# Piece sizes, half loads and an earlier first store in a DMA-bound DoRA forward kernel

## Chip, cores, metric

One NeuronCore of a Trainium2 chip. The metric is device microseconds of one execution. Before: 162.53 us, the median of 6 runs (162.31 to 163.03).

## The reference

```python
W_adapted = W + scale * (lora_A @ lora_B)          # 256 x 256, rank 16
W_norm = np.sqrt(np.sum(W_adapted ** 2, axis=0, keepdims=True) + 1e-8)
W_final = W_adapted / W_norm * m
y = x.reshape(-1, 256) @ W_final                   # x: 16 x 2048 x 256 float32
```

33.5 MB of x come in, 33.5 MB of y go out. The small algebra on W takes the first microseconds.

## The kernel before

x is 64 groups of 512 rows (J = 4 rows in each of 128 partitions, 4 KB of a partition). Eight groups are a block of 4 MB. There are eight blocks, but SBUF has room for five (XBUFS = 5). ScalarE writes a group's result over its x. So the program loads five blocks, then stores three (freeing three buffers), loads the last three, and stores the rest. Loads go out on SyncE's queue, stores on ScalarE's. For each pair of groups GpSimd rounds x to bf16 (`xb`), TensorE transposes it (`turned`), VectorE copies it out (`xt`), TensorE multiplies (`product`) and ScalarE copies the result (`x_sb<-y_ps`).

```python
    loads = [(0, 2), (2, 2), (4, CH - 4)] + units[1 : XBUFS - 1]    # (first group, groups)
    loads += [((XBUFS - 1) * CH, CH - 3)]
    loads += [(XBUFS * CH - 3 + c, 1) for c in range(3)] + units[XBUFS:]
    ...
    F = NBLK - XBUFS                                # 3
    G = F * CH                                      # 24
    stores = [(b * CH, CH, 21 + b) for b in range(F - 1)]           # (first group, groups, due after group)
    stores += [(G - CH, CH // 2, 24), (G - CH // 2, CH // 2, 24)]
    FIRST = len(stores)
    stores += [(G + c, 1, G + 3) for c in range(4)]
    stores += [(G + 4, CH - 4, 47)]
    ...
    for n in range(len(loads)):                     # SyncE
        if loads[n][0] == XBUFS * CH:
            for k in range(HALF + 1):               # wait for the stores that free the buffers
                nc.sync.wait_ge(sem(f"store{k}"), 16)
        ...
        load_x(n)
    ...
        if p == REST:                               # GpSimd pauses at pair 15
            nc.gpsimd.wait_ge(sem(f"store{HALF}"), 16)
```

"A piece" below is what one partition moves in one run of a DMA: a load of a whole block has pieces of 32 KB, one of a single group 4 KB. A DMA over 128 partitions is 128 pieces (1280 packets of 32 KB for the ten DMAs of whole blocks), 8 for each of the 16 DMA engines.

## Time and profile before

| | before |
|---|---|
| span of the profile | 161.3 us |
| DMA bytes, mean rate | 67.42 MB, 418 GB/s |
| busiest compute engine (PE) | 59% |
| rate while only loads or only stores run | 431 to 432 GB/s |
| first store issued, first store packet | 48.53 us, 52.63 us |

The row to look at is the DMA row of the page: it is at 8 or 9 from the second slice to the last but one. Then only two kinds of loss are left: a DMA engine that is idle, and bytes that move slower than 432 GB/s. The prediction shows the lines for both. Two more views of the kernel before are needed later. The timeline of its start (start us, duration us, engine, line, operation, tiles):

```profile
13.76 2.45 DVE L234 TENSOR_TENSOR w_final<-wam,rnorm 128x256 bf16<-128x256 f32 x2
13.82 2.11 POOL L197 CAST xb<-x_sb 128x2048 bf16<-128x2048 f32 x1 [2.43 <-DMA x_sb<-in_x_dram]
16.13 1.21 DVE L238 COPY xt<-xt_ps 128x1024 f32<-128x1024 f32 x1
...
18.60 0.63 PE L316 MATMUL y_ps<-w_final,xt 128*128 128x256 bf16 x2
```

and the issue of the first store, on ScalarE's queue:

```profile
48.53 0.37 ACTq L149 DMA_DIRECT2D out_dram<-x_sb  x1
```

The weights are ready at 16.2 us, the first product starts at 18.60. w_final takes 2.45 us because it collides with a cast of GpSimd.

### The profile page before, as it was taken

The numbers are of one execution on the slowest core, as the hardware profiler recorded it, in microseconds if no ns is written. First come the engines' busy times: TensorE is split into PE (matmuls) and PEld (weight loads), VectorE is DVE, ScalarE is ACT, GpSimd is POOL, SyncE is SP. The second block draws the span as 40 slices with busy tenths as digits, with TensorE's granted clock in tenths as the row PEclk, the third lists the DMA queues.
The fourth block names the chain that finished last, engine by engine and source line by source line (L and its number), as shares of the span: only waits on it lengthen the run. The fifth ranks groups of instructions, "written<-read, shape, count | busy, mean of one in ns | idle before, by whom it ended". The sixth has DMA issues, their size and how long they took to land. (4 is left out here: it accounts for less than half of the span.)

```text
span 161.3 us, 2012 instructions
## 1 busy us (share of the span) xinstructions
PE 95.2 (59%) x786; PEld 83.8 (52%) x786; DVE 46.6 (29%) x44; ACT 63.9 (40%) x67; POOL 62.9 (39%) x39
## 2 busy tenths in 40 slices
PE   0491899999999700000199999999999940000000
PEld 0160799999998600000179989989899930000000
DVE  0439635353635300000033535353445300000000
ACT  3010076868686520000027675856776850000000
POOL 1085339776764000000674479198676200000000
PEclk9999999999999995555559999999999998555555
DMA  4999999999899999989999999999999999999995
GB/s 163 427 455 459 390 504 406 390 488 423 374 412 361 511 423 390 473 374 451 427 482 414 386 463 421 407 433 433 422 484 419 406 479 414 400 479 423 386 443 228
DMA packets 4356, 67.42 MB, mean 418 GB/s; under 512 B 625, under 2 KB 642, under 8 KB 1666
## 3 DMA queue, kind: packets, MB, share of 16 engines
q1 hardware_dynamic: 2160, 33.82, 49.5%
q10 hardware_dynamic: 2194, 33.59, 48.7%
q14 instruction: 2, 0.02, 0.0%
HBM read 33.85 MB, written 33.55 MB: 418 GB/s over the span
## 5 line engine op out<-in xcount | busy, mean ns | idle before, releaser
L256 ACT COPY x_sb<-y_ps 128x1024 f32<-128x1024 f32 x64 | 62.0, 1014 | 60.0 <-PE y_ps L316 57.8
L197 POOL CAST xb<-x_sb 128x2048 bf16<-128x2048 f32 x32 | 60.4, 1900 | 61.3 <-DMA out_dram<-x_sb 27.7
L316 PE MATMUL y_ps<-w_final,xt 128*128 128x256 bf16 x512 | 63.6, 278 | 1.2 <-PEq L291 1.1
L238 DVE COPY xt<-xt_ps 128x1024 f32<-128x1024 f32 x32 | 39.2, 1224 | 72.6 <-PE xt_ps L302 72.6
L316 PEld LDWEIGHTS y_ps<-w_final,xt 128*128 128x128 bf16 x512 | 51.1, 100 | 8.5 <-issue 1.9
L302 PE MATMUL xt_ps<-identity,xb 128*128 128x128 f32 x264 | 37.0, 287 | 28.2 <-PEq L291 28.2
L302 PEld LDWEIGHTS xt_ps<-identity,xb 128*128 128x128 f32 x264 | 31.7, 148 | 30.3 <-issue 30.0
L283 PE MATMUL y_ps<-sq,ones 128*128 128x256 f32 x4 | 2.1, 674 | 1.6 <-DVE sq L223 1.6
L272 PE MATMUL y_ps<-identity,a_nat 128*16 128x128 f32 x2 | 0.6, 394 | 4.1 <-DMA a_nat<-in_lora_A_dram 4.1
L248 ACT ACTIVATE norm<-y_ps,eps_col 128x256 f32<-128x256 f32 x1 | 0.5, 473 | 5.8 <-PE y_ps L283 5.8
L234 DVE TENSOR_TENSOR w_final<-wam,rnorm 128x256 bf16<-128x256 f32 x2 | 2.5, 1266 | 0.0
L283 PEld LDWEIGHTS y_ps<-sq,ones 128*128 128x128 f32 x4 | 1.2, 326 | 2.3 <-DVE sq L223 2.1
L272 PEld LDWEIGHTS y_ps<-identity,a_nat 128*16 128x16 f32 x2 | 0.1, 88 | 4.1 <-issue 4.1
L246 ACT ACT_TABLE_LOAD x1 | 1.3, 1283 | 2.4 <-issue 2.4
L203 POOL MEMSET xb<- 128x2048 bf16 x1 | 1.8, 1804 | 0.7 <-PE xt_ps L302 0.7
L231 DVE RECIPROCAL rnorm<-norm 128x256 f32<-128x256 f32 x1 | 1.7, 1747 | 0.0
L225 DVE COPY m_all<-y_ps 128x256 f32<-128x256 f32 x1 | 0.4, 424 | 3.3 <-PE y_ps L288 3.3
L214 DVE CAST b_bf<-b_nat 16x256 bf16<-16x256 f32 x1 | 0.3, 281 | 3.5 <-DMA b_nat<-in_lora_B_dram 3.5
L288 PE MATMUL y_ps<-m_row,ones 1*128 1x256 f32 x2 | 1.2, 706 | 0.0
L276 PE MATMUL y_ps<-b_bf,aT 16*128 16x256 bf16 x2 | 0.6, 404 | 0.7 <-DVE aT L216 0.7
L219 DVE SCALAR_TENSOR_TENSOR wa<-y_ps,w_nat 128x512 f32<-128x512 f32 x1 | 0.7, 692 | 0.8 <-PE y_ps L276 0.8
L288 PEld LDWEIGHTS y_ps<-m_row,ones 1*128 1x128 f32 x2 | 0.5, 308 | 0.6 <-issue 0.6
(13 smaller groups left out, 3.3 us busy)
## 6 DMA issues: line engine op xcount, KB each, us to landing
x_sb<-in_x_dram SPq DMA_DIRECT2D x5, 4096.0 KB, 26.5
out_dram<-x_sb ACTq DMA_DIRECT2D x5, 4096.0 KB, 22.7
out_dram<-x_sb ACTq DMA_DIRECT2D x5, 2048.0 KB, 29.0
x_sb<-in_x_dram SPq DMA_DIRECT2D x3, 2048.0 KB, 31.4
x_sb<-in_x_dram SPq DMA_DIRECT2D x1, 2560.0 KB, 44.8
x_sb<-in_x_dram SPq DMA_DIRECT2D x2, 1024.0 KB, 6.1
out_dram<-x_sb ACTq DMA_DIRECT2D x4, 512.0 KB, 50.1
x_sb<-in_x_dram SPq DMA_DIRECT2D x3, 512.0 KB, 46.4
```

The costliest lines, as they stand in the source:

```text
L197: nc.gpsimd.tensor_copy(out=xb_bufs[p % NXB][:], in_=x_bufs[b % XBUFS][:, 2 * c * J : 2 * (c + 1) * J, :],).then_inc(sem("rounded"), 1)
L203: nc.gpsimd.memset(xb_bufs[NPR % NXB][:], 0.0).then_inc(sem("rounded"), 1)
L219: nc.vector.scalar_tensor_tensor(out=wa[:], in0=ab_ps, scalar=float(scale), in1=w_nat[:], op0=ALU.mult, op1=ALU.add).then_inc(dv, 1)
L231: nc.vector.reciprocal(out=rnorm[:], in_=norm[:]).then_inc(dv, 1)
L234: i = nc.vector.tensor_mul(out=w_final[:, t], in0=wam[:, t], in1=rnorm[:])
L238: nc.vector.tensor_copy(out=xt_bufs[p % NXT][:].rearrange("p r t -> p (r t)").bitcast(FP32), in_=xt_ps[p % 2][:],).then_inc(sem("copied"), 1)
L246: nc.scalar.activation(out=warm[:], in_=eps_col[:], func=AF.Sqrt)
L256: nc.scalar.copy(out=x_bufs[b % XBUFS][:, c * J : (c + 1) * J, :], in_=y_ps[g % 2][:]).then_inc(sem("room"), 1)
L283: i = nc.tensor.matmul(n2_ps, ones[:], sq[:, t, :], start=(t == 0), stop=(t == KC - 1))
L288: nc.tensor.matmul(mb_ps, ones[0:1, :], m_row[:], start=True, stop=True).then_inc(pe, 1)
L302: i = nc.tensor.transpose(xt_ps[p % 2][:, j * P : (j + 1) * P], xb_bufs[p % NXB][:, j, :].bitcast(FP32), identity[:],)
L316: i = nc.tensor.matmul(y_ps[h][:, j, :], xt_bufs[p % NXT][:, r : r + P, t], w_final[:, t, :], start=(t == 0 and (j % (J // 2)) == 0), stop ...
```

## The change

The intent: compute starts earlier (the first pair is rounded by ScalarE, m is broadcast before the norm, GpSimd stays out of VectorE's way), so that the first store can be issued earlier; loads arrive in halves so that compute waits less; and at the two places where loads and stores meet, one side is cut into 2 KB pieces so that it trickles between the large pieces of the other side. The diff, cut to its core (waits and helper functions left out):

```diff
-    loads = [(0, 2), (2, 2), (4, CH - 4)] + units[1 : XBUFS - 1]
-    loads += [((XBUFS - 1) * CH, CH - 3)]
-    loads += [(XBUFS * CH - 3 + c, 1) for c in range(3)] + units[XBUFS:]
+    H = XBUFS * CH
+    loads = [(0, 2, 2 * J), (2, 2, 2 * J), (4, 4, 4 * J), (8, 4, 4 * J), (12, 4, 4 * J)]
+    loads += [(b * CH, CH, CH * J) for b in range(2, XBUFS - 1)]
+    loads += [(H - CH, 4, 4 * J), (H - 4, 4, 2)]          # third number: rows of a piece, 1 KB each
+    loads += [(g0, 4, 4 * J) for g0 in range(H, NCH - 4, 4)]
+    loads += [(NCH - 4, 2, 2 * J), (NCH - 2, 2, 2 * J)]
-    stores = [(b * CH, CH, 21 + b) for b in range(F - 1)]
-    stores += [(G - CH, CH // 2, 24), (G - CH // 2, CH // 2, 24)]
+    stores = [(b * CH, CH, CH * J, 20 + b) for b in range(F - 1)]
+    stores += [(G - CH, 3, 3 * J, G - 1), (G - 5, 1, J, G - 1), (G - 4, 4, 4 * J, G - 1)]
-    stores += [(G + c, 1, G + 3) for c in range(4)]
-    stores += [(G + 4, CH - 4, 47)]
+    stores += [(G, 4, 2, G + 3), (G + 4, CH - 4, (CH - 4) * J, 49)]
...
-    for p in range(NPR):                                   # GpSimd
+    for p in range(1, NPR):
...
-        if p == 0:
-            nc.gpsimd.wait_ge(sem("dve"), 4)
+        if p == 1:
+            nc.gpsimd.wait_ge(sem("dve"), 6)
+        if p == 2:
+            nc.gpsimd.wait_ge(sem("dve"), 8)
...
+    nc.vector.wait_ge(dv, 8)
+    nc.vector.sem_inc(sem("room"), 2)                      # was done by TensorE
...
+    wait_load(nc.scalar, 0)
+    nc.scalar.copy(out=xb_bufs[0][:], in_=x_bufs[0][:, 0 : 2 * J, :]).then_inc(sem("early"), 1)
...
+    nc.tensor.matmul(mb_ps, ones[0:1, :], m_row[:], start=True, stop=True).then_inc(pe, 1)   # moved ahead of n2
     nc.tensor.wait_ge(dv, 4)
```

More of the change, by code (lines that the diff above doesn't have):

```diff
@@ L103, with pieces @@
     units += [(NCH - CH, CH // 2), (NCH - CH // 2, CH // 2)]
-    loads = [(0, 2), (2, 2), (4, CH - 4)] + units[1 : XBUFS - 1]
-    loads += [((XBUFS - 1) * CH, CH - 3)]
-    loads += [(XBUFS * CH - 3 + c, 1) for c in range(3)] + units[XBUFS:]
-    load_of = {g: n for n, (g0, cnt) in enumerate(loads) for g in range(g0, g0 + cnt)}
     F = NBLK - XBUFS
     G = F * CH
-    stores = [(b * CH, CH, 21 + b) for b in range(F - 1)]
-    stores += [(G - CH, CH // 2, 24), (G - CH // 2, CH // 2, 24)]
-    FIRST = len(stores)
-    stores += [(G + c, 1, G + 3) for c in range(4)]
-    stores += [(G + 4, CH - 4, 47)]
-    stores += [(b * CH, CH, max(47, (b + 1) * CH - 1)) for b in range(F + 1, NBLK - 1)]
-    stores += [(g0, cnt, g0 + cnt - 1) for g0, cnt in units[-2:]]
-    HALF = FIRST - 2
+    H = XBUFS * CH
[4 more added lines that the diff above has]
+    loads += [(NCH - 4, 2, 2 * J), (NCH - 2, 2, 2 * J)]
+    load_of = {g: n for n, (g0, cnt, _) in enumerate(loads) for g in range(g0, g0 + cnt)}
+    stores = [(b * CH, CH, CH * J, 20 + b) for b in range(F - 1)]
+    stores += [(G - CH, 3, 3 * J, G - 1), (G - 5, 1, J, G - 1), (G - 4, 4, 4 * J, G - 1)]
+    FIRST = len(stores)
+    stores += [(G, 4, 2, G + 3), (G + 4, CH - 4, (CH - 4) * J, 49)]
+    stores += [(b * CH, CH, CH * J, max(49, (b + 1) * CH - 1)) for b in range(F + 1, NBLK - 1)]
+    stores += [(g0, cnt, cnt * J, g0 + cnt - 1) for g0, cnt in units[-2:]]
+    def pieces(entry):
+        return 16 * (entry[1] * J // entry[2])
     late = [nc.alloc_semaphore(f"store{n}") for n in range(FIRST, len(stores))]
@@ L132, in sem, with transfer, wait_load, wait_store @@
         return sems[name]
-    def in_sbuf(g0, cnt):
+    def transfer(engine, name, entry, dram, store):
+        g0, cnt, rows = entry[:3]
         b, c = divmod(g0, CH)
-        return x_bufs[b % XBUFS][:, c * J : (c + cnt) * J, :]
-    def in_dram(dram, g0, cnt):
         (u0, ucnt), = [u for u in units if u[0] <= g0 < u[0] + u[1]]
         unit = dram[u0 * J * P : (u0 + ucnt) * J * P].rearrange("(p j) k -> p j k", p=P)
-        return unit[:, (g0 - u0) * J : (g0 - u0 + cnt) * J, :]
+        for r in range(0, cnt * J, rows):
+            here = x_bufs[b % XBUFS][:, c * J + r : c * J + r + rows, :]
+            there = unit[:, (g0 - u0) * J + r : (g0 - u0) * J + r + rows, :]
+            src, dst = (here, there) if store else (there, here)
+            engine.dma_start(out=dst, in_=src).then_inc(sem(name), 16)
     def load_x(n):
-        nc.sync.dma_start(
-            out=in_sbuf(*loads[n]), in_=in_dram(x_flat, *loads[n])
-        ).then_inc(sem(f"load{n}"), 16)
+        transfer(nc.sync, f"load{n}", loads[n], x_flat, False)
     def store_y(n):
-        nc.scalar.dma_start(
-            out=in_dram(out_flat, *stores[n][:2]), in_=in_sbuf(*stores[n][:2])
-        ).then_inc(sem(f"store{n}"), 16)
+        transfer(nc.scalar, f"store{n}", stores[n], out_flat, True)
+    def wait_load(engine, g):
+        engine.wait_ge(sem(f"load{load_of[g]}"), pieces(loads[load_of[g]]))
+    def wait_store(engine, n):
+        engine.wait_ge(sem(f"store{n}"), pieces(stores[n]))
     nc.sync.dma_start(
@@ L162 @@
     for n in range(len(loads)):
-        if loads[n][0] == XBUFS * CH:
-            for k in range(HALF + 1):
-                nc.sync.wait_ge(sem(f"store{k}"), 16)
-        if loads[n] == units[-1]:
-            nc.sync.wait_ge(sem(f"store{HALF + 1}"), 16)
+        if loads[n][0] == H:
+            for k in range(FIRST - 1):
+                wait_store(nc.sync, k)
+        if loads[n][0] == H + G - 4:
+            wait_store(nc.sync, FIRST - 1)
         load_x(n)
@@ L183 @@
     ).then_inc(sem("ident"), 1)
-    for p in range(NPR):
+    for p in range(1, NPR):
         b, c = divmod(p, PRB)
         for g in (2 * p, 2 * p + 1):
-            if g == 0 or load_of[g - 1] != load_of[g]:
-                nc.gpsimd.wait_ge(sem(f"load{load_of[g]}"), 16)
-        if p == 0:
-            nc.gpsimd.wait_ge(sem("dve"), 4)
+            if g == 2 or load_of[g - 1] != load_of[g]:
+                wait_load(nc.gpsimd, g)
+        if p == 1:
+            nc.gpsimd.wait_ge(sem("dve"), 6)
+        if p == 2:
+            nc.gpsimd.wait_ge(sem("dve"), 8)
         if p == REST:
-            nc.gpsimd.wait_ge(sem(f"store{HALF}"), 16)
+            wait_store(nc.gpsimd, FIRST - 3)
         if p >= NXB:
@@ L223 @@
     nc.vector.tensor_mul(out=sq[:], in0=wa[:], in1=wa[:]).then_inc(dv, 1)
-    nc.vector.wait_ge(sem("pe"), 4)
+    nc.vector.wait_ge(sem("pe"), 3)
     nc.vector.tensor_copy(out=m_all[:], in_=mb_ps).then_inc(dv, 1)
@@ L246 @@
     nc.scalar.activation(out=warm[:], in_=eps_col[:], func=AF.Sqrt)
-    nc.scalar.wait_ge(sem("pe"), 3)
+    wait_load(nc.scalar, 0)
+    nc.scalar.copy(out=xb_bufs[0][:], in_=x_bufs[0][:, 0 : 2 * J, :]).then_inc(
+        sem("early"), 1
+    )
+    nc.scalar.wait_ge(sem("pe"), 4)
     nc.scalar.activation(
@@ L258 @@
         ).then_inc(sem("room"), 1)
-        due = [n for n in range(len(stores)) if stores[n][2] == g]
+        due = [n for n in range(len(stores)) if stores[n][3] == g]
         if due:
@@ L279 @@
     i.then_inc(pe, 1)
+    nc.tensor.wait_ge(sem("load_m"), 16)
+    nc.tensor.matmul(mb_ps, ones[0:1, :], m_row[:], start=True, stop=True).then_inc(pe, 1)
     nc.tensor.wait_ge(dv, 4)
@@ L286 @@
     i.then_inc(pe, 1)
-    nc.tensor.wait_ge(sem("load_m"), 16)
-    nc.tensor.matmul(mb_ps, ones[0:1, :], m_row[:], start=True, stop=True).then_inc(pe, 1)
     def take(name):
@@ L298, in turned @@
     def turned(p):
-        take("rounded")
         for j in range(2 * J):
@@ L323, in product @@
             i.then_inc(sem("product"), 1)
+    nc.tensor.wait_ge(sem("early"), 1)
     turned(0)
-    nc.tensor.wait_ge(dv, 8)
-    nc.tensor.sem_inc(sem("room"), 2)
     with nc.Fori(0, NPR // 2, 1, engines=[PE], head_slot={PE: 128}):
+        take("rounded")
         turned(1)
         product(0)
+        take("rounded")
         turned(0)
@@ L338 @@
     tc.compile()
-    for s in late:
-        nc.sync.wait_ge(s, 16)
+    for k, s in enumerate(late):
+        nc.sync.wait_ge(s, pieces(stores[FIRST + k]))
         nc.sync.sem_clear(s)
```

## The prediction

> **What bounds the kernel now.** I began with the page of the profile: the busy shares, the 40 slices, the DMA totals.
>
> ```profile
> PE 95.2 (59%) x786; PEld 83.8 (52%) x786; DVE 46.6 (29%) x44; ACT 63.9 (40%) x67; POOL 62.9 (39%) x39
> ...
> DMA  4999999999899999989999999999999999999995
> ...
> DMA packets 4356, 67.42 MB, mean 418 GB/s; under 512 B 625, under 2 KB 642, under 8 KB 1666
> ```
>
> No compute engine is over 59% busy, while the DMA row is at 8 or 9 in every slice but the first and the last. The chain of waits that ended last begins at 113.31 us and ends in a DMA issue at 132.23 us; the other 29 us of the 161.3 us span are stores that drain. So the 16 DMA engines are the bound, in every stage. What can be won is time in which they are idle, or move bytes slower than their best.
>
> Then I cut the span into stretches (columns: engines' busy us, granted clock, DMA share, GB/s):
>
> ```profile
> 14.00:42.00 28.00, 25.14 (x217) 23.17 (x218) 14.36 (x12) 16.16 (x17) 18.61 (x10) 1.00 1.00 431
> 44.00:60.00 16.00, 11.52 (x103) 10.01 (x100) 5.13 (x5) 9.71 (x10) 4.78 (x3) 1.00 1.01 416
> 118.00:158.00 40.00, 13.03 (x120) 11.85 (x118) 4.90 (x4) 10.66 (x12) 5.73 (x4) 0.72 1.00 432
> 156.00:161.30 5.30, 0.00 (x0) 0.00 (x0) 0.00 (x0) 0.00 (x0) 0.00 (x0) 0.50 0.65 278
> ```
>
> Loads alone and stores alone both run at 431 to 432 GB/s. The stretch from 44 to 60 us, where the first 20 MB of loads end and the stores begin, runs at 416: (432 - 416)/432 x 16 us = 0.6 us lost. The DMA view of 46 to 57 us (slices of 0.275 us) shows where:
>
> ```profile
> GB/s 1117 0 298 894 0 521 670 0 209 432 417 387 432 417 402 417 402 328 194 298 298 268 328 402 1728 238 0 0 1221 715 0 0 357 1430 119 0 0 1430 477 0
> ```
>
> A packet counts where it starts, so large ones make the row jump, but two steps are plain. From slice 9 on, the last three loads (4 KB pieces) run at some 410. Then six slices from 50.7 to 52.3 us have a mean of 286: the handover to the stores, whose first 32 KB packets start at 52.6 us though the first store was issued at 48.53. From the packet records, with each packet's bytes spread over its duration, I get 404 GB/s over 48 to 51 and 324 over 51 to 53 us: 0.20 + 0.50 = 0.70 us lost there. That is nearly all that the middle holds. The rest of 161.3 - 67.42 MB / 432 GB/s = 5.2 us is the start (first packet at 2.0 us, then small weight transfers) and the end (the last store lands at 159.8 us on its first DMA engine and 161.2 on its last).
>
> **What the Trainium skill says.** "DMA: Bandwidth & Descriptors", section "Where 436 GB/s comes from", gives 435 GB/s as the ceiling of a core; 432 here agrees, so the steady stages hold nothing. The same page, "Why small descriptors are slow (HBM only)", charges a fixed cost to each packet. The records agree: 32 KB take 1213 ns, 16 KB 611, 8 KB 309, 4 KB 159 and 2 KB 84, and 1213/16 = 75.8, so a 2 KB piece costs 8 ns extra. Its section "Queues, rings and completion order" says that a DMA engine round-robins between the rings for which it has work. This agrees: from 82 to 102 us the 4 KB stores trickle out between 32 KB loads, issued at 57.7 to 60.3 us and landing between 91 and 117. "SBUF — State Buffer", section "Who interferes with whom", says that a VectorE instruction with two SBUF inputs and a GpSimd one that reads SBUF block each other. The two halves of w_final agree: 425 ns and 2108 ns, the second of them under the cast that ran from 13.82 for 2.11 us.
>
> **The change, part by part.**
>
> *Start of the compute.* ScalarE rounds pair 0 when load 0 lands (6.6 us); an estimate is 2 x 1013 ns from its copies of 1024 columns, so about 8.6 us. The m product precedes the norm and waits for m (6.4 us), so the norm moves by about 0.1 us, and m_all and the product with it leave the chain after the norm. GpSimd's casts wait for steps 6 and 8 of VectorE, so w_final should take 2 x 0.42 us instead of 2.5. Working through: n2 ends 9.75, norm 10.25, reciprocal 12.0, w_final 12.9, first xt copy at about 13 instead of 16.13, first product at about 14.3 instead of 18.39. None of this is on the path of the end, because the DMA engines are busy with loads until 50 us anyway. It only brings the first store forward.
>
> *Half loads.* Block 1 in halves lets GpSimd go on at about 18.6 instead of 23.54 us. But block 2 stays whole and lands at 33.2 us. Its cast ends at 35.1, and PE, at 2.62 us a pair, is then only 1.6 us ahead of before (36.7). Store 0 is due one group earlier too (group 20, not 21): with 2.62 us a pair, issue at about 46 us instead of 48.53. The latency to first packets was 4.1 us at this place (48.53 to 52.63), so stores flow from about 50. Cost: each 32 KB piece that becomes two of 16 KB costs 2 x 611 - 1213 = 9 ns; 8 per engine and block, blocks 1, 5, 6: 0.2 us at most, and 0.06 us for the last loads of 8 KB.
>
> *Last loads in 2 KB.* Groups 36 to 39 become 8 DMAs, 64 pieces of 2 KB a DMA engine. They begin at about 47.0 us. Alone they run at 16 x 2048 B / 84 ns = 390 GB/s: (432 - 390)/432 x 2.9 us = 0.28 us lost until the stores flow, with 34 of the 64 gone. The other 30 trickle, one to each 32 KB store piece, and are in by about 75 us; the program pauses at pair 15 until the third store lands, also about 75, and needs them only at pair 18. So no wait comes of it. Because the load ring is not dry when the stores arrive, I expect most of the 0.50 us of the handover to vanish: I count 0.10. Sum 0.38 instead of 0.70: -0.32 us.
>
> *First late stores in 2 KB.* Groups 24 to 27 take 64 pieces a DMA engine instead of 32. They trickle beside 40 loads of 16 KB and 16 of 8 KB. From 102 to 116 us, before, 16 KB and 4 KB alternated at 428 GB/s: 0.13 us lost over 35 packets, 3.7 ns each. For 2 x 56 packets that is 0.41 us, less the 0.16 us that this stage lost before: +0.25. The 30 trickling loads: 60 x 2 to 3.7 ns, +0.15. The eight issues block ScalarE for up to 8 x 1.1 us (the 1.10 us of those before), in a stretch where it waited 26 us in any case.
>
> Sum, counting half the cost of the half loads because mixed packets hide part of it: -0.32 + 0.25 + 0.15 + 0.1 = +0.2 us. That is less than the 0.7 us between the slowest and fastest run of before. As the 3.7 ns a packet is the softest term and I take it for somewhat too high (32 KB mixed with 4 KB lost almost nothing, 431.7 GB/s from 90 to 102 us), I put the change at 0.0: 162.6 us.
>
> **Rivals.**
> 1. *Small pieces cost their whole 8 ns also when mixed.* I count 128 more data packets a DMA engine (120 to 208 for loads, 112 to 152 for stores): 128 x 8 = 1.0 us, and with a handover as bad as before, 163.8. For it: the durations of single packets. Against it: the 431.7 GB/s just named.
> 2. *The handover and the skew shrink together.* With the load ring never dry, 0.6 us comes back, and the DMA engines end closer together: the last store's sixteen landings now lie 1.4 us apart, most of them within 0.5. Then 161.5. For it: most of that spread is already there at the landing at 118.4 us, after the mixed stage; against it: the change mixes more, not less.
> 3. *A new gap.* Loads 40 and on are issued only when four stores have landed, 3.7 us before their first packets (77.92 to 81.63). If the pieces queued behind ran out, DMA would idle. Before, 10 us of stores covered it (2 MB each of 16 KB and 4 KB pieces); after, the same bytes do, plus leftovers. Likewise stores due at group 49: I place them near 107 us, 9 us before the loads end. If that failed, PE would become the bound for a while: 165 to 167. I see no sign of it.
>
> **Range and chances.** Terms of 0.3 to 1.0 us with both signs on a kernel that is saturated over 97% of its span: 161.3 to 163.9 us. Faster by 2% means under 159.4 us. The engines would then have to lose 3.2 us less, while everything between start and end loses about 1.2; so 3%. Slower by 2% needs a gap of 3.3 us, rival 3 or slow HBM reads of 2 KB; 4%.
>
> **What would show it.** Right: xt's first copy near 13 us, w_final two times 0.42, ScalarE's first store issue near 46, 44 to 60 us at 420 GB/s or more, no DMA slice under 8 inside, total packets up by about 2050 of data. Wrong: a slice under 400 GB/s between 60 and 116 us (rival 1 or 3), or casts that wait for the loads of groups 36 to 39 past 82 us. The prediction fails as a whole if a DMA slice in the middle falls to 6 or lower.

## The result

163.56 us, the median of 6 runs (163.39 to 163.85), against 162.53 (162.31 to 163.03): the ratio is 1.0063, with a 95% interval of 1.0045 to 1.008. So "the same" by the 2% line, but clearly slower, by 1.0 us.

The page of the kernel after, the rows that answer to those of before:

```profile
PE 94.6 (58%) x786; PEld 83.6 (52%) x786; DVE 45.0 (28%) x44; ACT 65.8 (41%) x68; POOL 60.9 (38%) x38
...
DMA  4999999999999999999999999999999999999895
...
DMA packets 6372, 67.42 MB, mean 416 GB/s; under 512 B 849, under 2 KB 866, under 8 KB 3170
```

The same bytes, 2016 more packets, and no gap: DMA is busy all through. The compute part did most of what it was meant to do. The timeline of the start after:

```profile
6.43 1.90 ACT L262 CAST xb<-x_sb 128x2048 bf16<-128x2048 f32 x1 [2.56 <-DMA x_sb<-in_x_dram]
...
11.82 0.76 DVE L245 TENSOR_TENSOR w_final<-wam,rnorm 128x256 bf16<-128x256 f32 x2
12.72 2.35 DVE L252 COPY xt<-xt_ps 128x1024 f32<-128x1024 f32 x2
...
14.25 0.56 PE L333 MATMUL y_ps<-w_final,xt 128*128 128x256 bf16 x3 [2.15 <-PEq L309]
...
46.30 0.37 ACTq L147 DMA_DIRECT2D out_dram<-x_sb  x1
```

w_final takes 0.76 us instead of 2.45, the first product starts 4.35 us earlier, the first store is issued 2.23 us earlier. Some of this belongs to the two executions that were profiled and not to the change: without the collision the old program starts its first product at 16.3 us too, and the new one issued its first store at 48.1 in experiments 1 and 2. But the stretches (engines' busy us, clock, DMA share, GB/s) show that the handover got worse:

```profile
14.00:42.00 28.00, 25.95 (x221) 23.38 (x222) 11.19 (x10) 17.44 (x18) 18.57 (x10) 0.94 1.00 431
44.00:60.00 16.00, 10.24 (x91) 8.71 (x89) 4.90 (x4) 8.30 (x9) 4.64 (x3) 0.97 1.03 413
...
118.00:158.00 40.00, 10.57 (x97) 9.56 (x95) 3.67 (x3) 8.88 (x10) 4.07 (x3) 0.66 1.00 432
```

and the DMA view of 46 to 57 us (slices of 0.275 us) shows how:

```profile
GB/s 596 238 715 30 246 417 387 387 380 365 305 238 209 201 149 313 656 767 909 22 127 648 640 603 7 134 879 767 238 119 268 752 871 7 119 529 760 611 127 7
```

The first slice is number 0. After 380 GB/s in slice 8, the 2 KB loads fall from 305 in slice 10 (48.7 us) to 149 in slice 14 (to 50.1 us). The dip begins 2.4 us after the first store's issue and ends when that store's first packets start (50.62 us). Before, the same dip lay between 50.7 and 52.6 us, 2.2 us after the issue at 48.53.

**A ledger of the loss.** Large packets make such rows jump, so for all comparisons I used the packet records: each packet's bytes are spread over its duration, and for a given number of megabytes moved, the loss is the time at which they had moved minus megabytes / 432.2 GB/s (the rate of the stores alone from 60 to 75 us of the kernel before). The increase of that loss, stage by stage, in us:

| stage, by MB moved | before | after |
|---|---|---|
| 0 to 19 (start, loads alone) | 2.83 | 2.86 |
| 19 to 22 (handover, loads to stores) | 0.71 | 1.04 |
| 22 to 28 (stores) | -0.01 | 0.02 |
| 28 to 34 (stores, to the next loads) | 0.03 | 0.15 |
| 34 to 46 (loads with trickling stores) | 0.09 | 0.28 |
| 46 to 50 (back to stores) | 0.10 | 0.18 |
| 50 to 67.3 (stores alone) | 0.01 | 0.00 |
| sum | 3.77 | 4.54 |

So the engines lose 0.77 us more: 0.33 at the handover, 0.12 while the 2 KB loads trickle, 0.27 while the 2 KB stores do. The span grew by 0.76 (161.28 to 162.04). The remaining 0.3 us lie outside the span: time minus span is 1.3 us for the profiled run of before, and 1.6 us (median) after.

### The profile page after: what moved, and what is told of

It is laid out like the page before. It is cut to its first block, busy times and chain, and to the rows that moved or that the text cites. A ratio compares the mean times of both kernels' runs of the same rounds, so it can differ in the third digit from the quotient of the medians.

```text
span 162.0 us, 2026 instructions
## 1 busy us (share of the span) xinstructions
PE 94.6 (58%) x786; PEld 83.6 (52%) x786; DVE 45.0 (28%) x44; ACT 65.8 (41%) x68; POOL 60.9 (38%) x38
## 5 line engine op out<-in xcount | busy, mean ns | idle before, releaser
L207 POOL CAST xb<-x_sb 128x2048 bf16<-128x2048 f32 x31 | 58.4, 1893 | 60.9 <-DMA out_dram<-x_sb 28.0
L319 PE MATMUL xt_ps<-identity,xb 128*128 128x128 f32 x264 | 36.2, 283 | 25.9 <-PEq L309 25.9
L262 ACT CAST xb<-x_sb 128x2048 bf16<-128x2048 f32 x1 | 1.9, 1900 | 2.6 <-DMA x_sb<-in_x_dram 2.6
L239 DVE TENSOR_TENSOR wam<-wa,m_all 128x256 f32<-128x256 f32 x2 | 0.8, 421 | 0.0
```

What stands on the lines that cost most here:

```text
L207: nc.gpsimd.tensor_copy(out=xb_bufs[p % NXB][:], in_=x_bufs[b % XBUFS][:, 2 * c * J : 2 * (c + 1) * J, :],).then_inc(sem("rounded"), 1)
L262: nc.scalar.copy(out=xb_bufs[0][:], in_=x_bufs[0][:, 0 : 2 * J, :]).then_inc(sem("early"), 1)
L319: i = nc.tensor.transpose(xt_ps[p % 2][:, j * P : (j + 1) * P], xb_bufs[p % NXB][:, j, :].bitcast(FP32), identity[:],)
```

## The experiments

Each kernel ran 5 timed rounds, or 6 runs with the profiled one where that was counted, against the kernel before on the same chip. Issue times and losses are of one profiled execution of each kernel, so a difference of 0.1 or 0.2 us between two of them may be chance. The questions: is it the small pieces, and where? And why did the handover get worse, when the loads were meant to fill it?

**1. No 2 KB loads.** The changed kernel with

```diff
-    loads += [(H - CH, 4, 4 * J), (H - 4, 4, 2)]
+    loads += [(H - CH, 4, 4 * J), (H - 4, 4, 4 * J)]
```

> The changed kernel with the load of groups 36 to 39 as one DMA of 16 KB pieces instead of eight of 2 KB. Theory A (small load pieces cost the time at the handover): the bytes lost between 46 and 54 us fall from about 1.05 us to 0.3 or less, and the 0.15 us lost between 72 and 82 us goes too; time 162.5 to 162.8 against 163.56 for the changed kernel. Theory B (the switch of direction itself costs it, whatever the piece): the handover still loses 0.7 us or more, time 163.2 to 163.6.

Measured: 163.21 us (162.98 to 163.29), ratio 1.0035 to before. The handover lost 0.76 us, stage 28 to 34 MB 0.07 instead of 0.15. Theory A's second half holds (trickling 2 KB loads cost 0.1 us), its first half does not: the handover still lost as much as before the change. So both the loss and the time are as theory B forecast. But this run had issued its first store at 48.10, not 46.30, so a second quantity had moved, and not by the edit, whose load moves its data only from 47 us on. From 34 to 42 us TensorE's granted clock was 0.76 to 0.81 in this execution and 1.00 in the one of the kernel after; in experiment 2 it was 0.73 to 0.84. The issue time is that of an execution and not of a kernel.

**2. No 2 KB stores.**

```diff
-    stores += [(G, 4, 2, G + 3), (G + 4, CH - 4, (CH - 4) * J, 49)]
+    stores += [(G, 4, 4 * J, G + 3), (G + 4, CH - 4, (CH - 4) * J, 49)]
```

> The changed kernel with the store of groups 24 to 27 as one DMA of 16 KB pieces instead of eight of 2 KB. Theory A: the rate from 82 to 117 us rises from 425 to 428 GB/s to over 431, 0.25 to 0.4 us back, time 163.1 to 163.3. Theory B' (this stage is slow because the loads come in 16 KB halves): rate stays at 428 and the time at 163.5.

Measured: 163.37 us (163.28 to 163.45), ratio 1.005, a little over theory A's range. Stage 34 to 46 MB lost 0.08 us instead of 0.28: the cost of the 2 KB stores is real, and the 16 KB halves are not to blame, theory B' falls. Stage 46 to 50 lost 0.22, a short dip at 114.5 to 115.5 us that took part of the gain back: the rate from 82 to 102 us rose from 428.0 to 430.7 GB/s, but from 82 to 117 only to 428.7, not to 431. The first store was issued at 48.11, and the handover lost 0.85.

**3. Neither.** Both edits.

> Both: no 2 KB pieces at all, all else as in the changed kernel. Theory A, if the two costs add: 162.2 to 162.5, at or a little under the kernel before (162.53). If the 0.3 us that the changed kernel takes outside the span of the profile has another source than the pieces, 162.5 to 162.8. Theory B: 163.2 or more.

Measured: 163.16 us (162.97 to 163.34), ratio 1.0035. The stages from 28 to 50 MB lost 0.24 us against 0.22 before and 0.61 after: all of the cost of small pieces is gone there. But the handover lost 1.06 us, without a single 2 KB piece in it. Its first store was issued at 46.31, as in the changed kernel. So theory A falls for the handover. Theory B is right that the piece of the load is not the cause, but the loss is not constant either: it went 0.71, 0.76, 0.85, 1.04, 1.06 as the issue went 48.53, 48.10, 48.11, 46.30, 46.31.

**4. Only the compute part.** The kernel before's loads and stores, with all of the change to ScalarE, GpSimd, VectorE and TensorE.

> The kernel before with the compute part of the change alone: first pair by ScalarE, m ahead of the norm, GpSimd held back from w_final; loads and stores as before. All theories: first products near 14 us instead of 18.4, but block 1 whole still lands at 23.5, so the first store comes no more than 1 us earlier; time 162.3 to 162.7, same as before within 0.2 us. If it comes out over 162.9, the early start itself costs something.

Measured: 162.68 us (162.59 to 163.07), ratio 1.001, interval 0.9997 to 1.0023. The time is as expected, the reason is not. The first store was issued at 49.62 us, 1.1 us later than before. Compute starts early, runs out of data (block 1 is whole here) and TensorE's granted clock falls (0.62 from 26 to 30 us): its timeline shows a wait of 3.99 us, after which 16 matmuls take 2.75 us instead of 1.91:

```profile
19.71 1.91 PE L335 MATMUL y_ps<-w_final,xt 128*128 128x256 bf16 x16
25.61 1.94 PE L321 MATMUL xt_ps<-identity,xb 128*128 128x128 f32 x8 [3.99 <-PEq L311]
27.34 2.75 PE L335 MATMUL y_ps<-w_final,xt 128*128 128x256 bf16 x16
```

With this late store the handover has no dip at all, and loses 0.21 us. The DMA view of 46 to 57 us of this kernel; the first 32 KB store packets (1773) start as the last 4 KB loads end:

```profile
GB/s 1117 74 0 1192 0 298 894 0 179 417 387 417 447 373 417 432 432 343 417 462 357 417 1773 357 0 0 119 1787 0 0 0 1549 357 0 0 715 1192 0 0 0
```

By the ledger the handover is 0.5 us better than before, but the stage from 46 to 50 MB lost 0.35 us (0.10 before), a dip at 114 to 115.5 us. And time minus span is 1.6 us, as in every kernel so far that has the compute part.

From here on theory C: what costs the time is a store that starts while loads are still queued.

**5. The first store later, no 2 KB pieces.** Experiment 3 with

```diff
-    stores = [(b * CH, CH, CH * J, 20 + b) for b in range(F - 1)]
+    stores = [(b * CH, CH, CH * J, 22) for b in range(F - 1)]
```

> No 2 KB pieces, and the first two stores due at group 22 instead of 20 and 21, so the first is issued near 49 us (50.7 if PE loses its clock while it waits for block 2) instead of 46.3. Theory C (what costs the time is a store that starts while loads are still queued: loads slow down about 2.2 us after the issue, until the first store packet): the dip begins at 51 us or later and the loads end at 52, so the handover loses 0.0 to 0.4 us instead of 1.04; time 162.5 to 162.8 against 163.16. Rival D (the loss belongs to the switch and comes whenever the first store is issued): loss still about 1 us, time 163.1.

Measured: 162.98 us (six runs from 162.72 to 163.31, in two clusters), ratio 1.0023, which is slower than the 162.5 to 162.8 that theory C forecast. Issue at 49.05, and the handover lost 0.29 instead of 1.06, as theory C says; rival D falls. But of the 0.77 us won there the time shows 0.2: the profiled run, the slowest of the six (163.31), lost 0.38 in stage 34 to 46 (0.09 in experiment 3), 0.30 in 46 to 50 (0.10), and its DMA engines ended 2.0 us apart (1.66).

**6 and 7. The first store in smaller pieces.** Experiment 3 with the first store (block 0) in eight DMAs of 4 KB pieces, or two of 16 KB:

```diff
-    stores = [(b * CH, CH, CH * J, 20 + b) for b in range(F - 1)]
+    stores = [(b * CH, CH, CH * J if b else J, 20 + b) for b in range(F - 1)]        # 6; 4 * J in 7
```

> No 2 KB pieces, first store (groups 0 to 7) in 4 KB pieces instead of 32 KB, issued as early as in the changed kernel. Theory E (each DMA engine reads a whole store piece before it writes, and the loads starve for that time, so one 32 KB piece costs up to 1.2 us): loss at the handover falls from 1.04 to 0.3 us or less (4 KB is 0.16 us of an engine), plus up to 0.2 us for the small pieces after it; time 162.5 to 162.8. Rival F (the length of the dip, 2 us from the store's descriptors to its first packet, does not depend on the piece): the loss stays at 0.8 to 1.1 us, time 163.1 to 163.4.

> The same with the first store in 16 KB pieces. Theory E: loss about half, 0.5 to 0.6 us, time 162.7 to 162.9. Rival F: 1.0 us, time 163.1 to 163.2.

Measured: with 4 KB 163.58 us (163.29 to 164.36), with 16 KB 163.15 (163.04 to 163.46), against 163.16 with 32 KB. The handover lost 0.46 and 0.69 us instead of 1.06, so in the ledger the loss falls with the piece, as theory E says, though less than in proportion. Rival F's 0.8 to 1.1 us did not come. The time did not follow: all the 4 KB pieces after the handover lost 0.23 us in stage 22 to 28 and more later, and the 16 KB kernel gained nothing in the median (its profiled run lost 3.93 us in all, against 4.16 in experiment 3). As a way to a faster kernel it is a miss.

**8. The kernel before, only its first store earlier.**

```diff
-    stores = [(b * CH, CH, 21 + b) for b in range(F - 1)]
+    stores = [(b * CH, CH, 19 + 3 * b) for b in range(F - 1)]
```

> The kernel before with nothing changed but that its first store is due at group 19 instead of 21 (issued near 46 us instead of 48.53, with 4 KB load pieces last as before). Theory C: the loss at the handover grows from 0.71 to 1.0 us or a little more, time 162.8 to 163.0 against 162.6: an earlier store is worse, which no part of the compute or the 2 KB pieces can explain. Rival D: no change.

Measured: 163.12 us (163.00 to 163.14), ratio 1.0035, interval 1.0013 to 1.0057. Issue at 46.82, the handover lost 1.19 us instead of 0.71, and every other stage of the ledger is as before (28 to 50 MB: 0.18 against 0.22). The same DMA view of this kernel:

```profile
GB/s 1117 0 447 745 0 745 447 0 224 417 402 298 253 179 134 74 164 268 387 1072 775 74 74 119 1475 596 0 0 74 1475 596 0 0 89 1683 357 0 0 521 1445
```

From slice 11 (49.0 us, 2.2 us after the issue) to slice 17 the loads fall to 74 GB/s, and the first store packets start at 51.25. One number of the kernel was changed, nothing of the compute and no piece, and the time rose by 0.6 us, a little more than forecast. This is the cleanest evidence: an earlier store is a slower handover.

**9. The mirror: the kernel before, its first store later.**

```diff
-    stores = [(b * CH, CH, 21 + b) for b in range(F - 1)]
+    stores = [(b * CH, CH, 22) for b in range(F - 1)]
```

> The mirror of the earlier one: the kernel before with its first two stores due at group 22 instead of 21 and 22, issued near 50 us instead of 48.53. Theory C: the dip would begin at 52.2 us, when the 4 KB loads have landed, so the loss at the handover falls from 0.71 to 0.2 us. If the whole of it is kept, 162.0 to 162.1 against 162.5; if later handovers give back half of it, as the kernel with only the compute part and the one with later stores did, 162.2 to 162.4. If the time does not fall, theory C explains the profile of the handover but not the time.

Measured: 163.33 us in the median, and six runs from 162.36 to 163.96 (ratio 1.0056, interval 1.0034 to 1.0079). The profiled run is the fastest of them (162.36): issue at 49.63, handover 0.21 as expected, 0.47 lost in 46 to 50 MB (0.10 before). So where it goes well, its time is in the range forecast for half given back, but by the ledger nearly all is: 0.44 of the 0.50 us won (sum 3.71 against 3.77). Experiment 4 is alike (3.68). And in four of six runs something else goes wrong that I have no profile of. Theory C explains the handover of the profile, not the time of these runs. What happens in the slow ones stays open.

**10. Later, and no small pieces, on the kernel before.** Experiment 9 with block 4 as one load and groups 24 to 27 as one store:

```diff
-    loads += [((XBUFS - 1) * CH, CH - 3)]
-    loads += [(XBUFS * CH - 3 + c, 1) for c in range(3)] + units[XBUFS:]
+    loads += [((XBUFS - 1) * CH, CH)]
+    loads += units[XBUFS:]
...
-    stores += [(G + c, 1, G + 3) for c in range(4)]
+    stores += [(G, 4, G + 3)]
```

> The kernel before with the same later stores and no small pieces either: block 4 as one load of 32 KB pieces, groups 24 to 27 as one store of 16 KB. Handover loss 0.1 to 0.2 us, mixed stage 0.1 us better than before: 161.9 to 162.1 if kept, 162.2 to 162.4 if half is given back. It is the candidate that should beat both kernels. Without small pieces at the handover a rival would be a gap (loads end at 51.5 us, first store packets 2.6 us after the issue, 52.5): then no gain, 162.5.

Measured: 164.38 us (163.91 to 165.27), ratio 1.0131: a clear miss, and an instructive one. The first handover was perfect, it lost 0.01 us. But stage 34 to 46 lost 0.67 and 46 to 50 lost 1.52. The DMA rows of its page and of two stretches:

```profile
DMA  4999998998999999989999999999699999999796
...
112.00:116.00 4.00, 4.00 (x39) 3.77 (x38) 1.38 (x2) 3.31 (x4) 2.75 (x2) 1.00 0.94 401
116.00:118.00 2.00, 2.00 (x21) 1.83 (x19) 1.23 (x1) 0.35 (x1) 1.80 (x1) 1.00 0.51 213
...
116.46 1.82 ACTq L149 DMA_DIRECT2D out_dram<-x_sb  x3
```

There are real gaps (the 6 and the 7 inside the row). Without small pieces the 16 KB stores take about a third of the bytes from the loads of block 5 until they are done (135 of 393 GB/s from 84 to 92 us; the 4 KB stores of the kernel before took 48 of 441). Block 5 lands at 97.5 us instead of 93.8, compute is late, and the stores due at group 47 are issued at 116.46, when the loads have just ended. That is what the trickling pieces are for: they leave the loads their bandwidth. Experiment 3 has 16 KB stores as well, but its loads come in halves, and the first half of block 5 lands at 92.1; that this is why it shows no gap was not tested alone.

**11. Only the first pair on ScalarE.** The kernel before with the first pair's cast moved to ScalarE, and nothing else:

```diff
-    for p in range(NPR):
+    for p in range(1, NPR):
...
+    nc.scalar.wait_ge(sem("load0"), 16)
+    nc.scalar.copy(out=xb_bufs[0][:], in_=x_bufs[0][:, 0 : 2 * J, :]).then_inc(sem("early"), 1)
     nc.scalar.wait_ge(sem("pe"), 3)
```

> The kernel before with the first pair rounded by ScalarE and nothing else of the change. It asks where the 0.27 us come from by which the time exceeds the span of the profile in every kernel that has the compute part (1.5 to 1.6 us) and in none that lacks it (1.3 us). If the rounding on ScalarE causes it, time minus span is 1.5 to 1.6 us here; if the reordered m or the handing over of room by VectorE does, 1.3 us. Time 162.4 to 162.9 in either case.

Measured: 162.54 us (162.42 to 162.76), ratio 1.0004. Time minus span is 1.32 us, as before. So the 0.3 us outside the span do not come from ScalarE's cast; they come from the rest of the compute part (m ahead of the norm, GpSimd's waits, VectorE handing over `room`). Which of these, and how something before or after the profiled span comes of it, stays open. On the side, one more point for theory C: issue at 47.92, handover 0.88. (The kernel of experiment 12 issued at 47.89 without this edit, so the earlier issue is not shown to come from it.)

**12. The kernel before, its first store in 16 KB pieces.**

```diff
-    stores = [(b * CH, CH, 21 + b) for b in range(F - 1)]
+    stores = [(0, 4, 21), (4, 4, 21), (CH, CH, 22)]
```

> The candidate from the runs so far: the kernel before, issue times unchanged (first store at 48.53), with its first store in two DMAs of 16 KB pieces instead of one of 32 KB. Theory E says that the dip at the handover shrinks with the first store's piece (1.04 us with 32 KB, 0.67 with 16 KB, both issued at 46.3); here the loads end before the dip does, so 0.71 us become 0.45 to 0.6. Sixteen more pieces of 16 KB cost under 0.05 us. Time 162.2 to 162.4 against 162.5, if nothing is given back. If the loss at the handover stays at 0.7, the piece matters only when many loads are left.

Measured: 162.72 us (162.55 to 163.12), ratio 1.0016: not faster. Issue at 47.89 in the profiled run, and the handover lost 1.08, more than the 0.88 of experiment 11 with 32 KB pieces issued at the same time. This contradicts theory E. What the piece of the first store does stays open: with 16 KB loads waiting a smaller piece lost less (6 and 7), with 4 KB loads it lost more.

**All handovers together**, ordered by the issue of the first store (us; loss in stage 19 to 22 MB):

| kernel | issue | loads waiting | loss |
|---|---|---|---|
| after | 46.30 | 2 KB | 1.04 |
| 3 | 46.31 | 16 KB | 1.06 |
| 8 | 46.82 | 4 KB | 1.19 |
| 11 | 47.92 | 4 KB | 0.88 |
| 1 | 48.10 | 16 KB | 0.76 |
| 2 | 48.11 | 2 KB | 0.85 |
| before | 48.53 | 4 KB | 0.71 |
| 5 | 49.05 | 16 KB | 0.29 |
| 4, 9 | 49.62, 49.63 | 4 KB | 0.21 |
| 10 | 49.67 | 32 KB | 0.01 |

(All with 32 KB pieces in the first store.) Up to about 47 us the loss is full, some 1.1 us; from there it falls to nothing for an issue some 2.5 us before the loads run out, at 52.2 to 52.4. The size of the waiting loads adds 0.1 to 0.2 at most. The first store packets came 2.0 to 2.6 us after the issue where the loads had all but run out (experiments 4, 9, 10) and 3.9 to 4.7 us after it for an issue up to 48.53: about 2 us more, as long as the dip. No kernel beats the one before.

## Why the prediction was right, and where it was not

The verdict (the same within 2%) and the range hold: 163.56 lies in 161.3 to 163.9. The point, 162.6, is 1.0 us too low. The range was wide enough (2.6 us) to hold although the term that decided the sum had the wrong sign, so the verdict says little for the mechanism. Its steps, one by one:

- **DMA is the bound, and compute moves nothing but the first store.** Right. Its times hold: xt's first copy at 12.72 (13), first product 14.25 (14.3; the 18.39 of before is a weight load, its product started at 18.60), w_final 418 and 426 ns, first store at 46.30 (46). The last is partly luck, as two other executions with the same start issued it at 48.1.
- **"Because the load ring is not dry when the stores arrive, I expect most of the 0.50 us of the handover to vanish: I count 0.10."** This is the step that failed. The term was -0.32 us, it measured +0.33. I took the dip of before for the sign of a queue that runs dry. The trace of before already spoke against this: its last load packets of that stage ended at 54.08 us, after the first store packet (52.63). It is the opposite: the loads are slowed because a store has started beside them, and the more of them are still queued, the more is lost, up to some 1.1 us. Experiment 3 has the full loss without small pieces, experiment 8 adds half a microsecond to the kernel before by issuing the store earlier, and experiments 4, 9 and 10 have almost no loss where the loads were just ending. So what brought the first store forward is what made the handover worse: the early start, the half loads and the store due one group earlier together (with the compute part alone, experiment 4, it was issued later than before).
- **Trickling loads, +0.15.** Measured +0.12 (28 to 34 MB), gone in experiment 1 down to 0.04. Right.
- **2 KB stores, +0.25.** Measured +0.27 (34 to 50 MB: 0.46 against 0.19), and 0.19 again in experiment 3. Right. I then took these terms back by setting the sum to 0.0, because 3.7 ns a packet seemed too high. It was not.
- **Half loads, 0.1 to 0.26.** 0.02 by 18 MB; overstated.
- **Small pieces as rival 1.** I counted 128 more data packets a DMA engine; it is 112 (1792 more in all, from the packet records): the loads have 72 more, not 88. Nor is 163.8 the rival's own sum, as 162.53 already holds the bad handover: 162.53 + 128 x 8 ns is 163.6. That is the measured time, but not for the rival's reason: small pieces account for 0.39 of the 1.0 us.
- **ScalarE blocked for up to 8.8 us by the eight issues.** It was 22.7, from 55.97 to 78.67 us, but in its idle time, as foreseen.
- **Outside the span, +0.3.** Nowhere in the prediction, which read only the span.
- **The ceiling of 435 GB/s.** The same section of the Trainium skill also says that transfers between HBM and SBUF are bound by some 358 GB/s of a core. The 431 to 432 GB/s measured here decide: the ceiling that the prediction took is the one that fits.

The sum as measured: 0.33 + 0.12 + 0.27 + 0.03 (start) + 0.02 (22 to 28 MB) = 0.77 us of bytes, and 0.3 outside: 1.0 us. Of the signs I named, "44 to 60 us at 420 GB/s or more" came out at 413; no casts waited for groups 36 to 39, and no slice fell below 8, both as predicted.

Shown by experiments: the cost of the earlier store at the handover (3, 8, and 4, 5, 9, 10 the other way; in the measured time only by 8), of the trickling loads (1, 3) and of the trickling stores (2, 3), and that the 0.3 us come with the compute part but not with ScalarE's cast (4, 11). Not shown: why the loads are slowed. Theory E, that a DMA engine which reads a store piece has no read left for a load in that time, fits 6 and 7, and 12 speaks against it. Open: why gains at the first handover are mostly given back at later ones (4, 5, 9), and the slow runs of 9.

## What to carry to other kernels

When DMA is busy nearly throughout, don't ask who waits; plot bytes moved against the steady rate and see at which megabyte time is lost, because busy shares hide it. Where one queue hands over to the other, a transfer issued earlier is not free: in this kernel a store that started while loads were queued cost up to 1.1 us, and the best place was some 2.5 us before they ran out, although aiming there was not reliably faster in total. Small pieces are paid for by the packet, but they also decide who gets the bandwidth; take them away only after looking at what then arrives late.

## What the Trainium skill lacked or had wrong

- "DMA: Bandwidth & Descriptors", section "Specifications", has 512 B as the transfer from which the full rate is reached. Here pieces of 2 KB took 84 ns each, which over 16 engines is 390 GB/s, and of 4 KB 159 ns, 412 GB/s, against 432 GB/s with 32 KB; the DMA rows agree (380 to 387 in slices 6 to 8 of the kernel after, some 410 from slice 9 of the kernel before). Mixed with 16 KB pieces of the other direction they cost less than these durations say: 64 pieces of 2 KB a DMA engine in place of 32 of 4 KB cost 0.2 us from 34 to 46 MB (before against after, and experiment 3 against 1), where an estimate from the durations is 0.29.
- The same page, section "Issuing engines are not separate DMA queues", calls the issue time usually small relative to the DMA. With many pieces queued it was not. Eight DMAs of 256 KB held ScalarE's queue for 22.70 us, and sixteen loads SyncE's for 29.34 (ten took 4.85 before). ScalarE's first four took 0.3 to 0.6 us each and its last four 3.5 to 7.5, SyncE's eleventh to fifteenth 2.1 to 8.5; that a full queue held them is not shown. In the timeline of the kernel after:

```profile
1.36 29.34 SPq L147 DMA_DIRECT2D x_sb<-in_x_dram  x16
...
55.97 22.70 ACTq L147 DMA_DIRECT2D out_dram<-x_sb  x8
```

- No page has it that a store started beside queued loads slows them: 2.2 to 2.4 us after the issue, for about 2 us, with up to 1.19 us lost (experiment 8). Loads started beside stores, at 81.6 us of the kernel before, lost next to nothing by the ledger (0.04 us from 28 to 36 MB, which is from 68 to 87 us).
- No page explains a difference between measured time and profiled span that depends on the kernel: 1.3 us without, 1.6 us with the compute part of the change.
